# Turning the gated activations of a macaron block by transposing transfers instead of TensorE transposes

## The chip, the cores and the metric

The kernel runs on one core of one Trainium2 chip. The metric is the device time of one execution in microseconds (us). The engines are TensorE (PE, whose weight loads are listed apart as PEld), VectorE (DVE), ScalarE (ACT), GpSimd (POOL) and SyncE (SP, which only issues transfers here). Sixteen DMA engines move data for the queues of SP, POOL and ACT.

## The reference, cut to what matters

One layer of a streaming encoder, 256 tokens of 2048 features, all in float32. The residual stream passes through a first feed-forward, a recurrent middle part with two branches, a cross-attention and a second feed-forward, and a last norm:

```
x = x + 0.5 * swiglu(rms_norm(x, ffn1_norm), ffn1_w_up, ffn1_w_down)
...
x = x + 0.5 * swiglu(rms_norm(x, ffn2_norm), ffn2_w_up, ffn2_w_down)
return rms_norm(x, final_norm)

def swiglu(h, w_up, w_down):
    gate, up = jnp.split(h @ w_up, 2, axis=-1)
    return (jax.nn.silu(gate) * up) @ w_down
```

The change concerns only the two feed-forwards. The hidden width is 5632, so `w_up` has 11264 columns. `silu(gate) * up` is called the gated activations below.

## The kernel before, in words

**Numbers in two parts.** PE multiplies operands of a shortened float32 type. Each operand is therefore split into a high part, which ACT makes with a copy (line 155), and a low part, which DVE makes as the difference (line 156). A product is three matmuls: high by high (line 566), low by high (line 567) and high by low (line 569).

**The feed-forwards.** `ffn` works through 11 groups (g = 0 to 10) of 512 hidden features. A group is eight products ("steps") for the gate and up halves; most are of the kind "fast", in which seven accumulators in PSUM take products of sums and differences of weight blocks, 21 matmuls a step. In the second feed-forward every step is fast but the last two of group 0. When a group's products are done, ACT and DVE bring the seven accumulators together in two tiles of 128 partitions by 1024 (lines 653 to 665; `hid` and `hd` in the second feed-forward, one buffer each; the halves of a 2048 wide tile `ev` in the first). `activate` then makes the gated activations: ACT applies silu (line 599), DVE multiplies (line 600). They end in two blocks, `e0` for the first 128 tokens and `e3` for the other 128, tokens on partitions and 512 features along the row.

**The turn.** The down product needs them with features on partitions. `turn` (lines 602 to 613) takes eight blocks of 128 by 128 through PE (line 607, into two PSUM banks), and from each bank ACT copies a high part (line 611) and DVE makes a low part (line 612) into a tile `hidop`. `late` holds the calls that are to come later: a number n with each says after how many steps, the current one included, it is written into the program; `tick` counts at the end of every step. A turn is written with n = 4 (2 for g = 0).

**The order.** `ffn_order` gives the steps: the down products of two finished groups, four column blocks c of 512 for each, are mixed in behind the groups. Behind groups 1 and 2 stand two down products, behind each group from 3 on four, at the end eight for the groups 9 and 10. A down product of one c and one group is 24 matmuls, in two half steps of 12, one for each 128 tokens.

**What sets the order on the engines.** The kernel is written in one stream, and the framework's planner places each engine's instructions by its own costs and due times, so an engine can run an instruction somewhat earlier or later than it is written; where `issue_after` stands, not before a named one. Each engine then runs its own queue in order, and a waiting instruction holds all that stand behind it. Weight tiles are loaded by SP into `raw` buffers (lines 289 to 298), and prepared up to two steps ahead of use (`weights`, `prepare`); the high parts have three buffers of 2048 columns, and a fast step of the second feed-forward uses two of them. So ACT's split of a step's second tile waits until PE has let go of an earlier one.

**Other users of what the change touches.** `Operands.add` (line 397) makes the high and low parts of a normed block. The tile `hd` also serves as a throwaway output for the squares of the last norms (line 458), which come with the last down products.

Of the kernel before, what the change touches and what calls it, by code (L numbers as in the profile page):

```python
# [7 lines left out]

F32 = mybir.dt.float32
F32R = mybir.dt.float32r  # L10
ACT = mybir.ActivationFunctionType
ALU = mybir.AluOpType

P = 128
T = 256
# [46 lines left out]
def ffn_order(every=False):  # L62

    out = [("mixed" if p > 5 else "fast", 0, p) for p in range(8)] if every else first(0)
    down = [("down", 0, 1, c, 0) for c in range(4)]  # L70
    for g in range(1, NG):
        if every:
            out += [("fast", g, p) for p in (1, 3, 4, 0, 2, 5, 6, 7)]
        else:
            out += first(g)
        if g > 2 and g % 2:
            down = [("down", g - 2, 2, c, b) for c in range(4) for b in (g - 2, g - 1)]
        n = 2 if g < 3 else 4
        out, down = out + down[:n], down[n:]
    return out + [("down", NG - 2, 2, c, b) for c in range(4) for b in (NG - 2, NG - 1)]  # L80


def adds(name, e):
# [11 lines left out]
def block_kernel(ctx: ExitStack, tc: tile.TileContext, xT, xin, memT, vec, gfin, bgate, lruw, wu1, wd1, win, wv,  # L95
# [280 lines left out]
    class Operands:  # L376
# [13 lines left out]
        def add(self, src, gain=None):  # L390
            t = self.new()
            if gain is None:
                act.activation(t[:, :T], src, ACT.Copy)
                dve.tensor_tensor(out=t[:, T:], in0=src, in1=t[:, :T].bitcast(F32), op=ALU.subtract)
            else:
                act.activation(t[:, :T], src, ACT.Copy, scale=gain)
                dve.scalar_tensor_tensor(out=t[:, T:], in0=src, scalar=gain, in1=t[:, :T].bitcast(F32),
                                         op0=ALU.mult, op1=ALU.subtract)
            return t

# [89 lines left out]
    def turned(tile, which=range(2)):  # L490

        accs = [bank() for _ in which]
        for y, acc in zip(which, accs):
            for z in range(2):
                for t in range(2):
                    pe.transpose(acc[:, z * T + t * P:][:, :P], tile[:, t * 512 + (2 * y + z) * P:][:, :P], ident)  # L496
        return accs

    def normed(ops, c, gain):

        accs = turned(xt[c])
        for m in range(4):
            ops.add(accs[m // 2][:, m % 2 * T:][:, :T], col(gain, 4 * c + m))

# [77 lines left out]
    def ffn(name, pairs, sq, then, begin=(), sums=()):  # L584


        order = orders[name]
        uses = {}
        for e in order:
            if e[0] != "down":  # L590
                for i, (_, _, n) in enumerate(PRODUCTS[e[0]]):
                    uses.setdefault((e[1], n), []).append((e[2], i))
        hids, accs = {}, {}
        late = []
        rstd = None

        def activate(sg, gate, up, t):

            act.activation(sg, gate, ACT.Silu, scale=rstd[:, t:t + 1])
            dve.scalar_tensor_tensor(out=sg, in0=up, scalar=rstd[:, t:t + 1], in1=sg, op0=ALU.mult, op1=ALU.mult)  # L600

        def turn(g, hid):
            for y in range(2):
                acc = bank()
                for z in range(2):
                    for t in range(2):
                        pe.transpose(acc[:, z * T + t * P:][:, :P], hid[t][:, (2 * y + z) * P:][:, :P], ident)  # L607
                o = slot(F32R, "hidop")
                ov = o.rearrange("p (z s c) -> p z s c", z=2, s=2)
                av = acc.rearrange("p (z c) -> p z c", z=2)  # L610
                act.activation(ov[:, :, 0], av, ACT.Copy)
                dve.tensor_tensor(out=ov[:, :, 1], in0=av, in1=ov[:, :, 0].bitcast(F32), op=ALU.subtract)
                hids[2 * g + y] = o

        def tick():
            for i in range(len(late)):
                n, f = late.pop(0)
                if n > 1:
                    late.append((n - 1, f))
                else:  # L620
                    f()

        for at, e in enumerate(order):
            w = weights(name, *e)
            kind = e[0]
            following = order[at + 1][0] if at + 1 < len(order) else None
            if kind != "down":
                g, p = e[1:]
                fast = kind == "fast"
                products = []  # L630
                for i, (a, b, n) in enumerate(PRODUCTS["ready" if sums_ready(name, e) else kind]):
                    u = uses[g, n]
                    if u[0] == (p, i):
                        accs[n] = bank()
                    own, less = pairs[p]
                    products.append((accs[n], part(own, a, P) if a >= 0 else part(less, -1 - a, P), part(w[b // 4] if fast else w, b % 4, 512),
                                     u[0] == (p, i), u[-1] == (p, i)))
                three(products, 3 if adds(name, e) else 0, adds(name, e) and p == 6)
                last = at + 1 == len(order) or order[at + 1][1] != g or following == "down"
                ends = kind != "plain" and uses[g, 0][-1][0] == p  # L640
                if ends or last:
                    if ends or kind == "plain":
                        if "hid" in scoped:
                            ev = [scoped[n].tile([P, 1024], F32, name=n, tag=n) for n in ("hid", "hd")]
                            e0, e3, e1, e2 = (v[:, i:i + 512] for v in ev for i in (0, 512))
                        else:
                            ev = scoped["wide"].tile([P, 2048], F32, name="ev", tag="wide")
                            e0, e1, e2, e3 = (ev[:, i * 512:(i + 1) * 512] for i in range(4))
                        if rstd is None:
                            with tc.issue_after(done["high"]):  # L650
                                rstd = sq.rstd_tokens()
                if ends:
                    act.activation(e0, accs[0], ACT.Copy)
                    dve.tensor_tensor(out=e1, in0=accs[5], in1=e0, op=ALU.add)
                    dve.tensor_tensor(out=e2, in0=accs[4], in1=e1, op=ALU.add)
                if last:
                    if kind == "plain":
                        activate(e0, accs[0], accs[1], 0)
                        activate(e3, accs[3], accs[2], 1)
                    else:  # L660
                        for o, n, x in ((e0, 1, e0), (e1, 3, e1), (e1, 2, e1)):
                            dve.tensor_tensor(out=o, in0=accs[n], in1=x, op=ALU.add)
                        activate(e0, e0, e1, 0)
                        for o, n, x in ((e3, 6, e2), (e2, 3, e2)):
                            dve.tensor_tensor(out=o, in0=accs[n], in1=x, op=ALU.add)
                        activate(e3, e3, e2, 1)
                    late.append((4 if g else 2, lambda g=g, hid=(e0, e3): turn(g, hid)))
            else:
                first, n, c, block = e[1:]
                if block == first:  # L670
                    accs["down"] = [bank(), bank()]
                for t in range(2):
                    products = []
                    for k in range(4):
                        a = hids[2 * block + k // 2][:, k % 2 * 512:][:, :512]
                        products.append((accs["down"][t], (a[:, t * P:][:, :P], a[:, T + t * P:][:, :P]),
                                         part(w, k, 512), block == first and k == 0, block == first + n - 1 and k == 3))
                    three(products)
                    if block == first + n - 1:
                        o = xt[c][:, t * 512:(t + 1) * 512]  # L680
                        done["residual"] = dve.scalar_tensor_tensor(out=o, in0=accs["down"][t], scalar=0.5, in1=o,
                                                                    op0=ALU.mult, op1=ALU.add).ins
                        if block == NG - 1:
                            then(c, t)
            if sums:
                sums.pop(0)()
            if begin:
                begin.pop(0)()
            tick()


# [382 lines left out]
    late = []  # L1074
# [275 lines left out]
```

## Time and profile before

| | |
|---|---|
| median of 3 runs | 2417.07 us |
| lowest and highest | 2416.99 and 2417.82 us |
| profiled execution, its own time | 2418.76 us |
| its span | 2417.0 us |
| granted clock of PE | 0.999 |
| moved by the DMA engines | 684.33 MB |
| first feed-forward's last turn | at 642.2 us |
| second feed-forward's turns | from 1776.7 to 2359.3 us |

The profile is one execution on the chip. Its span runs from the first instruction to the last; the execution's own time is a little longer. Busy times are given for each engine with their share of the span. The page groups instructions by line, engine, operation and tiles; other views give the instructions of one stretch in order of time, busy times of a stretch, the waits by what ended them, and the chain of work that ended last, followed back from the end. In all of them a time is counted from the span's start.

### The profile page before, as it was taken

To read this page: it belongs to the slowest core of one execution; us is meant where nothing else is said; L and a number is where in the kernel's file an instruction comes from. 1 tells how busy PE (TensorE), PEld (TensorE's weight loads), DVE (VectorE), ACT (ScalarE), POOL (GpSimd) and SP (SyncE) were. 2 spreads that over 40 slices of the span, in tenths; PEclk is the share of its full clock that TensorE was granted. 3 is DMA by queue.
4 is the path that set the end of the run, shared out by engine and by line. 5 is a ranking of instruction groups with operands and counts; after the bars stand their busy time and mean duration, and the time that the engine had idled before them with its cause. 6 is when DMAs were issued, how large, how long until landed. Compare 5 with 4: busy or idle time off the path is not lost.

```text
span 2417.0 us, 30834 instructions
## 1 busy us (share of the span) xinstructions
PE 2405.1 (100%) x12116; PEld 2006.3 (83%) x12116; DVE 2044.6 (85%) x2275; ACT 1468.6 (61%) x1499; POOL 102.3 (4%) x166
## 2 busy tenths in 40 slices
PE   9999999999999999999999999999999999999998
PEld 8888888888888888888888888888888788888887
DVE  6999999999866878678876787777789999999995
ACT  8566777777654454476434555545676666666664
POOL 0000000000000000000000000000000000000000
PEclk9999999999999999999999999999999999999999
DMA  8578999999858776878989899876788877787773
GB/s 305 203 227 258 276 277 278 273 275 271 270 215 318 276 285 240 302 269 324 353 323 348 291 358 344 324 286 244 265 344 308 292 283 279 269 287 279 285 282 140
DMA packets 102386, 684.33 MB, mean 283 GB/s; under 512 B 11360, under 2 KB 11616, under 8 KB 29280
## 3 DMA queue, kind: packets, MB, share of 16 engines
q1 hardware_dynamic: 78192, 518.68, 57.5%
q0 software_dynamic: 23328, 162.54, 22.4%
q8 instruction: 95, 1.56, 0.2%
q10 hardware_dynamic: 720, 1.13, 0.1%
q14 instruction: 51, 0.42, 0.0%
HBM read 619.39 MB, written 62.91 MB: 282 GB/s over the span
## 4 chain that ended last, share of the span: by engine, by line
PE 97%; DVE 1%; ACT 1%; DMA 1%; issue 0%; ACTq 0%
PE acc L566 18%; PE acc L567 18%; PE acc L569 18%; PE acc L332 11%; PE acc L357 8%; PE acc L358 8%; PE acc L360 8%; PE acc L335 6%; PE acc L607 1%; PE acc L496 1%; ACT h L155 1%; DVE l L156 0%; PE acc L904 0%; DMA raw<-wd 0%; PE acc L1197 0%; PE acc L1151 0%
## 5 line engine op out<-in xcount | busy, mean ns | idle before, releaser
L155 ACT ACTIVATE h<-raw 128x2048 fp32r<-128x2048 f32 (+3 forms) x578 | 867.6, 1526 | 618.8 <-PE acc L358 209.5
L156 DVE TENSOR_TENSOR l<-raw,h 128x2048 fp32r<-128x2048 f32 (+2 forms) x406 | 833.8, 2056 | 209.3 <-ACT h L155 206.3
L566 PE MATMUL acc<-h,xh 128*128 128x512 f32 x1228 | 478.4, 392 | 0.5 <-ACT h L155 0.5
L567 PE MATMUL acc<-h,xl 128*128 128x512 f32 x1228 | 476.1, 390 | 0.0
L357 PE MATMUL acc<-h,ops 128*128 128x512 f32 x832 | 326.8, 393 | 0.0
L358 PE MATMUL acc<-h,ops 128*128 128x512 f32 x832 | 324.6, 390 | 0.0
L332 PE MATMUL acc<-ops,h 128*128 128x512 f32 x1152 | 278.0, 393 | 0.0
L566 PE MATMUL acc<-h,hidop 128*128 128x512 f32 x704 | 276.3, 392 | 1.5 <-ACT h L155 1.5
L566 PEld LDWEIGHTS acc<-h,xh 128*128 128x128 f32 x1228 | 230.5, 188 | 54.4 <-ACT h L155 6.2
L567 PE MATMUL acc<-h,hidop 128*128 128x512 f32 x704 | 274.4, 390 | 0.0
L567 PEld LDWEIGHTS acc<-h,xl 128*128 128x128 f32 x1228 | 230.6, 188 | 46.7
L332 PEld LDWEIGHTS acc<-ops,h 128*128 128x128 f32 x1152 | 211.6, 188 | 41.6
L156 DVE TENSOR_TENSOR tl<-raw,h 128x1024 fp32r<-128x1024 f32 x172 | 203.7, 1220 | 13.8 <-ACT h L155 13.3
L360 PE MATMUL acc<-l,ops 128*128 128x512 f32 x832 | 205.8, 389 | 0.0
L155 ACT ACTIVATE h<-td 128x1024 fp32r<-128x1024 f32 x140 | 146.6, 1055 | 82.6 <-DVE td L304 31.5
L569 PE MATMUL acc<-l,hidop 128*128 128x512 f32 x704 | 190.5, 389 | 0.0
L360 PEld LDWEIGHTS acc<-l,ops 128*128 128x128 f32 x832 | 156.2, 188 | 32.4
L357 PEld LDWEIGHTS acc<-h,ops 128*128 128x128 f32 x832 | 156.2, 188 | 32.3
L358 PEld LDWEIGHTS acc<-h,ops 128*128 128x128 f32 x832 | 156.3, 188 | 31.5
L569 PE MATMUL acc<-tl,xh 128*128 128x512 f32 x624 | 178.1, 392 | 0.1
L156 DVE TENSOR_TENSOR tl<-td,h 128x1024 fp32r<-128x1024 f32 x140 | 170.1, 1220 | 8.3 <-ACT h L155 7.4
L569 PE MATMUL acc<-l,xh 128*128 128x512 f32 x604 | 166.5, 390 | 0.0
(245 smaller groups left out, 2750.5 us busy)
## 6 DMA issues: line engine op xcount, KB each, us to landing
raw<-wu SPq DMA_DIRECT2D x114, 1024.0 KB, 6.3
raw<-wd SPq DMA_DIRECT2D x88, 1024.0 KB, 6.5
prep<-wu POOLq DMA_DIRECT2D x58, 1024.0 KB, 6.5
t<-prep POOLq DMA_DIRECT2D x58, 1024.0 KB, 5.7
raw<-t SPq DMA_DIRECT2D x58, 1024.0 KB, 7.1
raw<-wu SPq DMA_DIRECT2D x58, 768.0 KB, 4.8
raw<-win SPq DMA_DIRECT2D x40, 1024.0 KB, 4.9
raw<-wg SPq DMA_DIRECT2D x32, 1024.0 KB, 5.1
```

The lines of the kernel that those rows point to most:

```text
L155: done["high"] = act.activation(h, raw, ACT.Copy).ins
L156: done["low"] = dve.tensor_tensor(out=l, in0=raw, in1=h.bitcast(F32), op=ALU.subtract).ins
L332: pe.matmul(acc, h[:, k * P:(k + 1) * P], xs[k], start=k == 0, stop=False)
L335: done["product"] = pe.matmul(acc[:, :T], l[:, k * P:(k + 1) * P], xs[k][:, :T], start=False, stop=k == KT - 1).ins
L357: pe.matmul(accs[t], x[:, t * P:][:, :P], h[j], start=first and j == 0, stop=False)
L358: pe.matmul(accs[t], x[:, T + t * P:][:, :P], h[j], start=False, stop=False)
L360: done["product"] = pe.matmul(accs[t], x[:, t * P:][:, :P], l[j], start=False, stop=last and j == 3).ins
L496: pe.transpose(acc[:, z * T + t * P:][:, :P], tile[:, t * 512 + (2 * y + z) * P:][:, :P], ident)
L566: pe.matmul(acc, ah, bh, start=start, stop=False)
L567: pe.matmul(acc, al, bh, start=False, stop=False)
L569: pe.matmul(acc, ah, bl, start=False, stop=stop)
L607: pe.transpose(acc[:, z * T + t * P:][:, :P], hid[t][:, (2 * y + z) * P:][:, :P], ident)
```

## The change

The turn of twelve groups, all eleven of the second feed-forward and g = 10 of the first, no longer goes through PE. In its place stand three parts. `planes` is an ACT copy that treats the two blocks as 2048 16-bit numbers a partition and parts them: first all low halves, then all high halves. `across` is one transposing transfer, issued on ACT's queue, of the 128 by 2048 16-bit numbers: each 128 by 128 block is turned. It goes from the second tile back into the first. `turned_planes` is an ACT copy that joins the halves to float32 numbers in the second tile, and then the same high parts (ACT) and low parts (DVE) as in `turn`, read from that tile and not from PSUM. `planes` and `across` are written at the end of the group's last step (n = 1), `turned_planes` with n = 6. In the first feed-forward the order of the four blocks in `ev` changes, so that `e0` and `e3` lie side by side.

`Operands.add` gets a view of its tile with more dimensions; the bytes are the same. `normed` may take its blocks from a turn begun earlier, but `begun_turns` is empty here, and `begin_turn` and `end_turn` are not called.

```diff
+BY_DMA = {"ffn1": range(10, 11), "ffn2": range(0, 11)}
...
-                act.activation(t[:, :T], src, ACT.Copy, scale=gain)
-                dve.scalar_tensor_tensor(out=t[:, T:], in0=src, scalar=gain, in1=t[:, :T].bitcast(F32),
+                tv = t.rearrange("p (s t n) -> p s t n", s=2, t=2) if len(src.shape) > 2 else t.rearrange(
+                    "p (s n) -> p s n", s=2)
+                act.activation(tv[:, 0], src, ACT.Copy, scale=gain)
+                dve.scalar_tensor_tensor(out=tv[:, 1], in0=src, scalar=gain, in1=tv[:, 0].bitcast(F32),
...
+    def planes(a, b):
+
+        act.activation(b.bitcast(U16).rearrange("p (two n) -> p two n", two=2),
+                       a.bitcast(U16).rearrange("p (n two) -> p two n", two=2), ACT.Copy)
+
+    def across(a, b):
+
+        act.dma_start_transpose(a.bitcast(U16).rearrange("p (i n) -> p i n", n=P), b.bitcast(U16))
...
+        def turned_planes(g, a, b):
+            act.activation(b.bitcast(U16).rearrange("p (n two) -> p two n", two=2),
+                           a.bitcast(U16).rearrange("p (two n) -> p two n", two=2), ACT.Copy)
+            bv = b.rearrange("p (t k n) -> p k t n", t=2, k=4)
+            for y in range(2):
+                o = slot(F32R, "hidop")
+                ov = o.rearrange("p (z s t n) -> p z s t n", z=2, s=2, t=2)
+                act.activation(ov[:, :, 0], bv[:, 2 * y:2 * y + 2], ACT.Copy)
+                dve.tensor_tensor(out=ov[:, :, 1], in0=bv[:, 2 * y:2 * y + 2], in1=ov[:, :, 0].bitcast(F32),
+                                  op=ALU.subtract)
+                hids[2 * g + y] = o
...
-                            e0, e1, e2, e3 = (ev[:, i * 512:(i + 1) * 512] for i in range(4))
+                            e0, e3, e1, e2 = (ev[:, i * 512:(i + 1) * 512] for i in range(4))
+                            ev = ev[:, :1024], ev[:, 1024:]
...
-                    late.append((4 if g else 2, lambda g=g, hid=(e0, e3): turn(g, hid)))
+                    if g in BY_DMA[name]:
+                        late.append((1, lambda ev=ev: planes(*ev)))
+                        late.append((1, lambda ev=ev: across(*ev)))
+                        late.append((6, lambda g=g, ev=ev: turned_planes(g, *ev)))
+                    else:
+                        late.append((4 if g else 2, lambda g=g, hid=(e0, e3): turn(g, hid)))
```

More of the change, by code (lines that the diff above doesn't have):

```diff
@@ L10 @@
 F32R = mybir.dt.float32r
+U16 = mybir.dt.uint16
 ACT = mybir.ActivationFunctionType
@@ L497, in turned, with begin_turn, end_turn @@
         return accs
-    def normed(ops, c, gain):
-        accs = turned(xt[c])
+    def planes(a, b):
[3 more added lines that the diff above has]
+        act.dma_start_transpose(a.bitcast(U16).rearrange("p (i n) -> p i n", n=P), b.bitcast(U16))
+    def begin_turn(tile, free=False):
+        a = slot(name="planes")
+        b = tile if free else slot(name="across")
+        planes(tile, a)
+        across(b, a)
+        return b, a
+    def end_turn(b, a):
+        act.activation(a.bitcast(U16).rearrange("p (n two) -> p two n", two=2),
+                       b.bitcast(U16).rearrange("p (two n) -> p two n", two=2), ACT.Copy)
+        v = a.rearrange("p (t k n) -> p k t n", t=2, k=4)
+        return [v[:, k] for k in range(4)]
+    begun_turns = {}
+    def normed(ops, c, gain):
+        if gain in begun_turns:
+            parts = end_turn(*begun_turns.pop(gain))
+        else:
+            accs = turned(xt[c])
+            parts = [accs[m // 2][:, m % 2 * T:][:, :T].rearrange("p (t n) -> p t n", t=2) for m in range(4)]
         for m in range(4):
-            ops.add(accs[m // 2][:, m % 2 * T:][:, :T], col(gain, 4 * c + m))
+            ops.add(parts[m], col(gain, 4 * c + m))
     BOTH = [0, 2, 4, 6]
@@ L666, in ffn @@
                         activate(e3, e3, e2, 1)
-                    late.append((4 if g else 2, lambda g=g, hid=(e0, e3): turn(g, hid)))
+                    if g in BY_DMA[name]:
+                        late.append((1, lambda ev=ev: planes(*ev)))
+                        late.append((1, lambda ev=ev: across(*ev)))
+                        late.append((6, lambda g=g, ev=ev: turned_planes(g, *ev)))
+                    else:
+                        late.append((4 if g else 2, lambda g=g, hid=(e0, e3): turn(g, hid)))
             else:
```

## The prediction, made before the changed kernel was run

> **What bounds the kernel now.** I read the page's busy shares first, then the stretch of the second feed-forward in the windows view, then who PE waits for there, and last the chain of work.
>
> ```profile
> PE 2405.1 (100%) x12116; PEld 2006.3 (83%) x12116; DVE 2044.6 (85%) x2275; ACT 1468.6 (61%) x1499; POOL 102.3 (4%) x166
> ```
> ```profile
> 1780.00:2340.00 560.00, 557.92 (x2485) 458.20 (x2484) 515.66 (x479) 364.03 (x319) 6.07 (x7) 1.00 0.80 289
> ```
> ```profile
> PE acc L566 <- ACT h L155: 2.0, 3, 1.2
> ```
>
> The second row is one stretch: its length, then busy time of PE, PEld, DVE, ACT, POOL, then clock, DMA share and GB/s. PE is idle for 560.00 - 557.92 = 2.1 us of 560, and what it waits for (third row, from 1680 us to the end) is the split of a weight tile into its high part by ACT. The reader is to see two things. Every PE instruction taken away shortens this stretch at once. And the engines behind PE have little to give: DVE is busy for 516 of 560 us, ACT for 364, the DMA engines for 0.80.
>
> **What the change removes.** Twelve groups (g = 10 of the first feed-forward, all eleven of the second) lose their eight PE transposes each.
>
> ```profile
> 642.35 0.87 PE acc L607 x8
> ```
> ```profile
> 1987.90 0.91 PE acc L569 x4
> 1990.62 0.91 PE acc L569 x4
> 1994.23 0.91 PE acc L569 x4
> 1996.95 0.91 PE acc L569 x4
> 2001.03 1.59 PE acc L569 x7
> 2005.79 1.59 PE acc L569 x7
> 2366.62 0.91 PE acc L569 x4
> 2369.34 0.91 PE acc L569 x4
> ```
>
> In the chain one turn takes 0.87 us. The second fence gives the same: the half steps of the down products end 2.72 us apart (1987.90 to 1990.62), and 3.61 us apart where the turn lies between them. So PE is relieved of 12 x 0.87 = **10.4 us**, all of it on the path. Each turn also frees two PSUM banks; PE's waits name no bank, so I count nothing for that.
>
> **What it adds on ACT and DVE.** Per group: one copy that parts the 16-bit halves (2048 elements a partition), one transfer issued on ACT's queue, one copy that joins the halves (2048 again), and the two operand copies and two DVE differences as before, from SBUF and not from PSUM.
>
> ```profile
> L273 ACT ACTIVATE l<-raw 128x2048 fp32r<-128x2048 f32 x18 | 34.3, 1907 | 2.0 <-PE acc L569 2.0
> L611 ACT ACTIVATE hidop<-acc 128x512 fp32r<-128x512 f32 x44 | 24.0, 587 | 3.8 <-PE acc L607 3.6
> L155 ACT ACTIVATE xh<-xg 128x512 fp32r<-128x512 f32 x16 | 10.1, 634 | 0.4
> L612 DVE TENSOR_TENSOR hidop<-acc,hidop 128x512 fp32r<-128x512 f32 x44 | 28.6, 684 | 0.9 <-ACT hidop L611 0.7
> L156 DVE TENSOR_TENSOR xl<-xg,xh 128x512 fp32r<-128x512 f32 x16 | 10.9, 689 | 12.4 <-ACT xh L155 12.4
> ```
>
> No row shows a 16-bit copy. ACT's 128x2048 copy takes 1.9 us; 16-bit elements could halve that (0.95) or the stride could double it (3.8); I take 1.9, the row with the same count. The operand copy moves from 587 to 634 ns, the DVE difference from 684 to 689: nothing. ACT gains 2 x 1.9 + 0.1 = 3.9 us a group, 47 us in all, on an engine that is busy 61% of the time. The view strides in the norm's operand helper name the same bytes as before: nothing.
>
> **Where that lies.** ACT runs its queue in order, so what stands behind the new instructions matters. This is ACT and DVE at the end of an ordinary group (bracket: idle before it), with the windows of the same place:
>
> ```profile
> 1981.60 1.31 ACT L599 ACTIVATE hid<-hid,rtok 128x512 f32<-128x512 f32 x2
> 1985.27 1.49 ACT L155 ACTIVATE h<-raw 128x1536 fp32r<-128x1536 f32 x1 [2.35 <-issue]
> 1990.70 2.01 ACT L155 ACTIVATE h<-raw 128x1024 fp32r<-128x1024 f32 x2 [3.95 <-PE acc L567]
> 1992.62 1.07 ACT L611 ACTIVATE hidop<-acc 128x512 fp32r<-128x512 f32 x2
> 1997.04 1.49 ACT L155 ACTIVATE h<-raw 128x1536 fp32r<-128x1536 f32 x1 [3.35 <-issue]
> 2004.02 3.39 ACT L155 ACTIVATE h<-raw 128x1024 fp32r<-128x1024 f32 x3 [1.37 <-PE acc L567]
> ```
> ```profile
> 1982.61 1.41 DVE L600 SCALAR_TENSOR_TENSOR hid<-hd,rtok,hid 128x512 f32<-128x512 f32 x2
> ```
> ```profile
> 1984.00:1998.00 14.00, 14.00 (x68) 11.68 (x67) 9.34 (x11) 5.43 (x6) 0.00 (x0) 1.00 1.00 347
> 1998.00:2030.00 32.00, 32.00 (x143) 26.48 (x142) 31.65 (x27) 22.16 (x20) 0.00 (x0) 1.00 0.66 241
> 2045.00:2106.00 61.00, 61.00 (x274) 50.06 (x273) 57.21 (x55) 39.37 (x34) 0.87 (x1) 1.00 0.77 271
> ```
>
> The new wait: the halves can be parted only when DVE's L600 has ended, at 1984.0. ACT stood idle from 1982.9 to 1985.3 anyway. Parting runs to 1985.9, the issue follows. Behind it are queued the split at 1985.27 and the pair at 1990.70, for products that start at 1996.95 + 0.91 = 1997.86 (after the change about 1997.0). The first split takes 1.49, the pair 2.01, and the pair is used six matmuls (6 x 0.227 = 1.36) later: ACT must be back by 1998.36 - 3.50 = 1994.9. **That is 8.5 us of room after the issue at about 1986.4.** ACT is busy for only 5.4 of these 14 us, and 1.07 of that, the operand copies, moves out.
>
> The joining copy is written after the first product of the next group, which ends about 1997.0 + 4.76 (2001.03 to 2005.79) = 2001.8. There ACT has 1.37 us idle in each 4.76 us product. The 1.9 + 1.27 us bunched there (before: 1.07, elsewhere) are made up within three products; the pair that they push back has 1.36 us of the product's start and the idle 1.37 for cover. Without that cover it would be up to 0.5 us a group. DVE is the tighter engine: 31.65 busy of 32. What ACT withholds from it for longer than DVE's idle 3.8 us in a group (61.00 - 57.21), PE pays.
>
> **The transfer.** 512 KB from SBUF to SBUF, its issue and its landing. No transposing transfer is in the trace.
>
> ```profile
> 1986.24 0.33 SPq L294 DMA_DIRECT2D raw<-wu  x1
> ```
> ```profile
> bgate<-bgate SPq DMA_DIRECT2D x4, 512.0 KB, 6.1
> mem<-memT SPq DMA_DIRECT2D x4, 512.0 KB, 9.7
> ```
> ```profile
> l<-wd POOLq DMA_DIRECT2D x1, 1024.0 KB, 13.0
> ```
>
> An issue costs 0.33 us in SP's row; landing takes 6.1 to 9.7 us for this size, and 13.0 us for the slowest transfer between 1984 and 2045 (last row). The windows say why the upper end counts: in the 14 us behind a group's end the DMA share is 1.00. I take 0.5 us for the issue and 8 us to land: 1994.4, and 1999.4 at 13 us, both before the joining copy wants it (2001.8). ACT's queue is behind neither SP's nor POOL's, but all three share the engines: 512 KB at the 347 GB/s of that window is 1.5 us of all engines, so the weight loads there slip by about that. The next window, at 0.66, takes it up.
>
> The Trainium skill speaks against the change: "VectorE: DVE Perf Modes", section "The three transpose paths", gives 390 ns for a 128x128 16-bit transpose on TensorE and 1309 ns by transfer. By it sixteen blocks, one after another, would be an estimated 21 us and land near 2007, after the joining copy wants it: the late form of the second rival. This case's TensorE row, 0.87 us for eight in a stream, is far below its 390 ns each, so by this trace its figures fit single operations, not a stream of them, and I give the late form a quarter of that rival's chance.
>
> **The last groups.** There the operands are wanted soonest.
>
> ```profile
> 2349.61 1.40 DVE L600 SCALAR_TENSOR_TENSOR hid<-hd,rtok,hid 128x512 f32<-128x512 f32 x2
> ```
>
> Ready at 2351.0; parted 2352.9, issued 2353.4, landed 2361.4 (2366.4 at 13 us), joined, copied and first difference made 1.9 + 0.63 + 0.69 = 3.2 us later: 2364.6 (2369.6). Wanted when the tenth half step ends, 2369.34 + 0.91 - 0.87 = 2369.4. Hidden, at the upper end just not. The first feed-forward's last group has the same shape.
>
> **The sum.** 10.4 us gained. ACT's 47 us, the transfers and their waits are hidden where I can place them. For the small slips I take as much as PE already waits in that stretch, 2.1 us; bounds 0 and 5 (0.5 a group). Net 8.3 us. The profiled execution took 2418.76 us round its span of 2417.0; it is 1.7 above the median 2417.07. From it: 2410.5; from the median: **2408.8 us**.
>
> **Rivals.**
> 1. *The gain is given back* (no change). DVE at 57.2 of 61 us becomes the bound in each group: ACT's bunched copies starve it and PE then waits for a low part. For it: the 31.65 of 32. Against it: DVE idles 4.7 us in the 14 us before, just where most of ACT's new work lies. At 0.9 us a group over ten groups: 2417.07 - 10.4 + 9 = about 2416.
> 2. *ACT's queue is held by the transfer* (slower), at the issue while its descriptors wait for saturated DMA engines, or at the joining copy because it lands late. Place: behind each group's end. It decides from 8.5 us of holding; beyond that PE stands one for one. If ACT comes back only when the engines are free, at 1998, that is 3.1 us a group, and over the ten groups 0 to 9: 2417.07 - 10.4 + 31 = about 2438. Groups 0 to 2 have fewer or no down products behind them and would pay more. If it is only late at the joining copy, say after twice the slower row of its size, 2 x 9.7 = 19.4 us, it lands at 2005.8; ACT stands 4.0 us, of which 1.37 + 1.36 are covered: 1.3 us a group, 2417.07 - 10.4 + 13 = about 2420. For it: DMA share 1.00 there, and no row for such a transfer. Against it: the issue of a weight load into that same window is 0.33 us in SP's row, and 13 us still lands in time.
>
> **Chances.** Forecast 0.60, rival 1 0.15, rival 2 0.25. What a measurement of this kernel can tell from no change is about 0.2%, 4.8 us: 2412.2 to 2421.9. A little of rival 1 falls below 2412.2: faster 0.62, same 0.13, slower 0.25. Low end: the whole 10.4 and a little PSUM ease, 2405. High end into rival 2, halfway between its two forms, 2429; beyond that 0.16 is left out, below 2405 0.03. The forecast's own range is 2405 to 2412.
>
> **What would show it.** PE's instructions fall from 12116 to 12020 and the L607 group from 176 to 80. ACT's busy time rises by about 47 us: a rise of 23 or 94 would show the 16-bit copies mis-sized. An ACT queue with twelve transposing transfers appears; median landing above 15 us, or ACT idle for over 8.5 us behind them, speaks for rival 2. PE's idle time between 1780 and 2340 rising from 2.1 to about 11 us would be rival 1, with DVE named as releaser. I am wrong if PE's waits for L155 grow by more than 5 us.

## The result, and the profile after

The changed kernel takes **2558.23 us** (median of 4 runs, 2552.32 to 2567.66) against 2417.23 us for the kernel before beside it (4 runs, 2416.99 to 2417.82): a ratio of 1.0587 [1.0551, 1.0622], 141 us slower. The profiled execution took 2561.84 us round a span of 2560.0. In the changed kernel's lines, the split of weights is L159 and L160 (before L155, L156), the three matmuls are L602, L603 and L605 (before L566, L567, L569), and the turn through PE is L643. New are L507 (parting copy), L512 (transposing transfer), L652 (joining copy), L658 and L659 (operand copies and differences).

The page of the changed kernel: span, busy times, packets, ACT's queue (q10: packets, MB, share of 16 engines), chain by engine.

```profile
span 2560.0 us, 30659 instructions
...
PE 2428.5 (95%) x12020; PEld 2010.2 (79%) x12020; DVE 2043.5 (80%) x2275; ACT 1516.8 (59%) x1523; POOL 102.3 (4%) x166
...
DMA packets 127345, 690.60 MB, mean 270 GB/s; under 512 B 36320, under 2 KB 36576, under 8 KB 54240
...
q10 hardware_dynamic: 25680, 7.43, 3.2%
...
PE 72%; DMA 12%; DVE 8%; ACT 5%; issue 3%; DVEq 0%; ACTq 0%; SPq 0%
```

PE has lost its 96 transposes (12116 to 12020), but the span has grown by 143.0 us. That splits in two: PE stands for 2560.0 - 2428.5 = 131.5 us, 119.6 more than before (2417.0 - 2405.1 = 11.9), and it is *busy* for 23.4 us more, with fewer instructions. The chain names who is waited for: DMA has 12% of it. The page before has q10 with 720 packets and 11360 packets under 512 B; now there are 24,960 more of both, 2080 small packets for each of the twelve transfers (0.52 MB, so some 250 B each).

The stretch of the second feed-forward that the prediction showed, in the windows view of the changed kernel:

```profile
1780.00:2340.00 560.00, 478.52 (x2006) 382.92 (x2005) 429.40 (x402) 340.14 (x286) 5.22 (x6) 0.93 0.83 250
```

PE was busy for 557.92 of these 560 us; now it is idle for 81. All of PE, DVE and ACT do less in the same time, and the DMA engines are busier (0.83 for 0.80) but move less (250 GB/s for 289). Who waits for whom, over the whole run of the changed kernel (total, times, longest):

```profile
PEld acc L602 <- ACT h L159: 114.9, 52, 20.3
...
PE acc L602 <- ACT h L159: 96.6, 24, 19.9
...
ACT hd L652 <- DMA hid<-hd: 80.3, 10, 19.2
...
ACT h L159 <- issue: 62.0, 15, 11.3
```

PE waits for ACT's weight splits (96.6 us against 2.0); ACT in turn stands at the joining copy until the transfer has landed, and at the issue. The total of that last row has not grown (69.8 us in 26 waits before), only its longest wait, from 3.5 us to 11.3. One group (g = 5), on ACT's timeline of the changed kernel (ACTq is ACT's sequencer, which issues the transfer):

```profile
2101.47 1.91 ACT L507 ACTIVATE hd<-hid 128x2048 uint16<-128x2048 uint16 x1 [1.47 <-DVE hid L636]
2103.29 1.47 ACT L159 ACTIVATE h<-raw 128x1536 fp32r<-128x1536 f32 x1
2103.41 9.36 ACTq L512 DMA_TRANSPOSE hid<-hd  x1
2112.89 2.01 ACT L159 ACTIVATE h<-raw 128x1024 fp32r<-128x1024 f32 x2 [8.13 <-issue]
2134.11 2.48 ACT L652 ACTIVATE hd<-hid 128x2048 uint16<-128x2048 uint16 x1 [19.21 <-DMA hid<-hd]
...
2137.68 3.36 ACT L159 ACTIVATE h<-raw 128x1536 fp32r<-128x1536 f32 x3
```

The issue holds ACT's queue for 9.36 us, not 0.5. The planner has put the joining copy only two places behind it, with one pair of splits between. There ACT stands for 19.21 us, and behind it stand the next weight splits. Over all groups, the tile's view and the transfer's landing in the changed kernel:

```profile
L512 ACTq DMA_TRANSPOSE hid<-hd x11: 1902/8921/16497, 1795.1 to 2490.4; - x11
...
DMA to landing us min/median/max: 6.8/17.2/31.8
```

The hold is 1.9, 8.9 and 16.5 us (least, median, most). The landing after 30.7 us in the group shown is one of the long ones; the median is 17.2. The last piece of the reading is what the transfer does to the loads beside it. The DMA view of that group's 31 us (103 to 134 us behind 2000) in the changed kernel:

```profile
q1 hardware_dynamic: 480, 3.20, 65.2%
q10 hardware_dynamic: 2080, 0.52, 28.2%
...
raw<-t SPq DMA_DIRECT2D x1, 1024.0 KB, 24.3
raw<-wu SPq DMA_DIRECT2D x1, 1024.0 KB, 19.0
raw<-wu SPq DMA_DIRECT2D x1, 768.0 KB, 19.8
hid<-hd ACTq DMA_TRANSPOSE x1, 30.7
```

SP's weight loads, 5.4 to 7.1 us over the run, took 19 to 24 us here. So the wait has two candidate causes. **Theory A**, the prediction's second rival: ACT's queue is held, at the issue and at the join. **Theory B**: the small packets of one queue and the large packets of another share the DMA engines badly, so the transfer and the loads are both late, and PE would starve even if ACT never stood. What the operation costs on engines alone (the copies) is a third.

### The profile page after: what moved, and what is told of

The parts are those of the page before. It is cut to its first block, busy times and chain, and to the rows that moved or that the text cites. A ratio compares the mean times of both kernels' runs of the same rounds, so it can differ in the third digit from the quotient of the medians.

```text
span 2560.0 us, 30659 instructions
## 1 busy us (share of the span) xinstructions
PE 2428.5 (95%) x12020; PEld 2010.2 (79%) x12020; DVE 2043.5 (80%) x2275; ACT 1516.8 (59%) x1523; POOL 102.3 (4%) x166
## 2 busy tenths in 40 slices
DMA packets 127345, 690.60 MB, mean 270 GB/s; under 512 B 36320, under 2 KB 36576, under 8 KB 54240
## 3 DMA queue, kind: packets, MB, share of 16 engines
q10 hardware_dynamic: 25680, 7.43, 3.2%
## 4 chain that ended last, share of the span: by engine, by line
PE 72%; DMA 12%; DVE 8%; ACT 5%; issue 3%; DVEq 0%; ACTq 0%; SPq 0%
PE acc L602 10%; PE acc L336 10%; PE acc L603 10%; PE acc L605 10%; DMA hid<-hd 7%; PE acc L361 7%; PE acc L362 7%; PE acc L364 7%; PE acc L339 5%; DVE tl L160 3%; ACT h L159 2%; DMA raw<-wd 2%; DVE l L160 2%; DMA raw<-t 1%; DMA ev<-ev 1%
## 5 line engine op out<-in xcount | busy, mean ns | idle before, releaser
L159 ACT ACTIVATE h<-raw 128x2048 fp32r<-128x2048 f32 (+3 forms) x578 | 865.2, 1525 | 607.5 <-PE acc L362 202.1
L160 DVE TENSOR_TENSOR l<-raw,h 128x2048 fp32r<-128x2048 f32 (+2 forms) x406 | 833.0, 2055 | 224.4 <-ACT h L159 222.4
L602 PE MATMUL acc<-h,xh 128*128 128x512 f32 x1228 | 490.4, 402 | 97.2 <-ACT h L159 94.2
L603 PE MATMUL acc<-h,xl 128*128 128x512 f32 x1228 | 484.5, 397 | 0.0
L602 PEld LDWEIGHTS acc<-h,xh 128*128 128x128 f32 x1228 | 235.8, 192 | 163.5 <-ACT h L159 109.7
L602 PE MATMUL acc<-h,hidop 128*128 128x512 f32 x704 | 279.2, 397 | 19.0 <-ACT hidop L658 16.4
L603 PE MATMUL acc<-h,hidop 128*128 128x512 f32 x704 | 277.7, 394 | 0.0
L603 PEld LDWEIGHTS acc<-h,xl 128*128 128x128 f32 x1228 | 236.1, 192 | 48.0
L160 DVE TENSOR_TENSOR tl<-raw,h 128x1024 fp32r<-128x1024 f32 x172 | 203.1, 1217 | 55.2 <-ACT h L159 55.2
L605 PE MATMUL acc<-l,hidop 128*128 128x512 f32 x704 | 193.1, 394 | 4.3 <-DMA l<-wd 3.5
L159 ACT ACTIVATE h<-td 128x1024 fp32r<-128x1024 f32 x140 | 146.6, 1054 | 82.2 <-DVE td L308 27.9
L605 PE MATMUL acc<-tl,xh 128*128 128x512 f32 x624 | 180.0, 393 | 1.5 <-DVE tl L160 1.4
L160 DVE TENSOR_TENSOR tl<-td,h 128x1024 fp32r<-128x1024 f32 x140 | 169.8, 1218 | 9.6 <-ACT h L159 8.8
L602 PEld LDWEIGHTS acc<-h,hidop 128*128 128x128 f32 x704 | 134.1, 190 | 49.9 <-ACT hidop L658 17.3
```

What stands on the lines that cost most here:

```text
L159: done["high"] = act.activation(h, raw, ACT.Copy).ins
L160: done["low"] = dve.tensor_tensor(out=l, in0=raw, in1=h.bitcast(F32), op=ALU.subtract).ins
L602: pe.matmul(acc, ah, bh, start=start, stop=False)
L603: pe.matmul(acc, al, bh, start=False, stop=False)
L605: pe.matmul(acc, ah, bl, start=False, stop=stop)
```

## The experiments

Each stands beside runs of the kernel before on the same chip: 2417.89, 2417.45 and 2418.21 us in the three sets (1 to 4, 5 to 8, 9 to 12).

**1. The copies alone.** `across` is not called; the join reads the parted tile.

```diff
-                        late.append((1, lambda ev=ev: across(*ev)))
-                        late.append((6, lambda g=g, ev=ev: turned_planes(g, *ev)))
+                        late.append((6, lambda g=g, ev=ev: turned_planes(g, ev[1], ev[0])))
```

> The transfer is left out, the two 16-bit copies stay: the halves are parted into the second tile and joined back into the first, so the activations are not turned (part of the computation left out). Theory (the transfer costs it all, by holding ACT's queue): 2407 to 2411 us, the forecast without the transfer. Rival (ACT's added 3.9 to 4.4 us a group starve DVE): over 2417, up to 2558.

Measured: 2412.70 us (2411.83 to 2414.28), 0.9977 [0.9967, 0.9987], a little above the 2407 to 2411 of the theory. Without the transfer nothing is lost, and 5 us are gained. All that the change loses comes with the transfer and its waits; ACT's 48 us of copies are hidden.

**2. The same bytes, not transposed.** A plain transfer of the same tile on the same queue.

```diff
-        act.dma_start_transpose(a.bitcast(U16).rearrange("p (i n) -> p i n", n=P), b.bitcast(U16))
+        act.dma_start(a.bitcast(U16), b.bitcast(U16))
```

> A plain transfer of the same 512 KB from the second tile to the first, on ACT's queue, in place of the transposing one (so nothing is turned). Theory (it is the transposing transfer's 2080 small packets): 2408 to 2420 us, landing 4 to 9 us. Rival (any 512 KB on ACT's queue at this place, while the DMA engines are saturated, holds it): over 2500.

Measured: 2424.77 us (2421.24 to 2426.35), 1.0025 [1.0016, 1.0034], above the 2408 to 2420 expected and far from the rival's 2500. The DMA view, the queue and the join's wait:

```profile
hid<-hd ACTq DMA_DIRECT2D x11, 512.0 KB, 8.1
```
```profile
ACT hd L652 <- DMA hid<-hd: 17.1, 8, 3.4
```

The prediction's 8 us to land is right for a plain transfer. Even that comes a little late where the planner joins: 17.1 us of waiting. It costs 12 us over the copies alone; the transposing form costs 146.

**3. The transfer aside.** PE turns as before the change; the parting copy and the transposing transfer on ACT's queue run too, behind PE's turn, and nobody uses their result.

```diff
-                        late.append((1, lambda ev=ev: across(*ev)))
-                        late.append((6, lambda g=g, ev=ev: turned_planes(g, *ev)))
+                        late.append((3, lambda g=g, ev=ev, hid=(e0, e3): (turn(g, hid), across(*ev))))
```

> TensorE turns as before (written at n = 3), the halves are parted, and the transposing transfer is issued on ACT's queue right behind the turn, but nothing reads its result. So the issue's hold on ACT and the load on the DMA engines stay, the wait for the landing goes. If the wait at the join were all (95 us of ACT's waits): 2417 to 2425. If the hold at the issue (median 8.9 us) and the slowed weight loads carry part of it: 2440 to 2520.

Measured: 2479.49 us (2470.38 to 2493.92), 1.0257 [1.0220, 1.0295]: 62 us with no wait at the join. One instruction still waited for a landing: a later user of the buffer of `ev`, on DVE (last fence; PE's longest wait from then to 720 us was 6 us). The profiled execution is the slowest of the four, 2493.92 us. From 1780 us to the end, in ACT's waits:

```profile
ACT h L159 <- issue: 35.1, 5, 9.6
ACT h L159 <- DMA raw<-t: 31.0, 8, 14.0
...
ACT h L159 <- DMA raw<-wu: 21.8, 5, 11.8
```
```profile
DVE S L937 <- DMA ev<-ev: 16.5, 1, 16.5
```

ACT has five waits of up to 9.6 us at the issue (before: 15 of up to 3.5 us, 42.7 in all), and it stands for 53 us because these weight tiles have not come (10.7 before, from 1680 us on). So not the join alone is at fault. Both theories have a row here.

**4. The transfer on SP's queue**, where the weight loads are.

```diff
-        act.dma_start_transpose(a.bitcast(U16).rearrange("p (i n) -> p i n", n=P), b.bitcast(U16))
+        sp.dma_start_transpose(a.bitcast(U16).rearrange("p (i n) -> p i n", n=P), b.bitcast(U16))
```

> As the changed kernel, but SP issues the transposing transfers, so the hold at the issue falls on the weight loads' queue and not on ACT. If the hold on ACT is the main cost: 2430 to 2490, with ACT free behind the parting copy. If the late landing at the join, or the slowed weight loads, are the main cost: 2540 to 2600.

Measured: 2435.33 us (2433.59 to 2438.27), 1.0067 [1.0050, 1.0083]. One word takes back 123 of the 141 us. The DMA view and the tile's view of this kernel:

```profile
hid<-hd SPq DMA_TRANSPOSE x11, 7.2
```
```profile
L512 SPq DMA_TRANSPOSE hid<-hd x11: 1692/5105/6841, 1780.8 to 2376.3; - x11
```

ACT is no longer held, as theory A wants. But the same transfer also lands in 7.2 us instead of 17.2, which A does not explain: it now stands in one line with the loads. The next set separates the two.

**5. ACT's queue, but the join late.** The join is written at n = 8 (6 in the last group), and `issue_after` holds it behind the latest split, so that the planner can't put it forward.

```diff
-                        late.append((6, lambda g=g, ev=ev: turned_planes(g, *ev)))
+                        def join(g=g, ev=ev):
+                            with tc.issue_after(done["high"]):
+                                turned_planes(g, *ev)
+                        late.append((8 if g < NG - 1 else 6, join))
```

> As the changed kernel (transfer on ACT's queue), but the joining copy is written at n = 8 (6 for the last group) and kept behind ACT's newest weight split, so that ACT reaches it some ten instructions after the issue instead of two. Its 95 us of waits for the landing should fall below 15. If that wait was the cost: 2412 to 2425. If the hold at the issue and the weight loads slowed by sharing the DMA engines carry most of it, as in the run where nobody read the result (2479): 2455 to 2500.

Measured: 2513.13 us (2504.8 to 2522.39), 1.0403 [1.0374, 1.0431], above both ranges. Waits of this kernel:

```profile
DVE raw L308 <- DMA raw<-wu: 37.4, 8, 14.6
...
ACT ev L652 <- DMA ev<-ev: 22.5, 1, 22.5
...
ACT hd L652 <- DMA hid<-hd: 2.1, 1, 2.1
```

The second feed-forward's wait at the join is gone (80.3 to 2.1 us), and only 45 us of the 141 come back. Other waits take its place: DVE now stands for weight loads, and the one join of the first feed-forward stands for 22.5 us.

**6. SP's queue and the join late** (edits 4 and 5 together).

> SP issues the transfers, and the joining copy is late as in the run before this one. On SP's queue the transfer landed in 7.2 us, and ACT waited 38.8 us for it at the join. If that early join is what is left of the loss (2435): 2410 to 2419. If it is the weight loads that stand behind the transfer on SP's queue: 2428 to 2438 again.

Measured: 2430.37 us (2429.02 to 2434.91), 1.0054 [1.0041, 1.0067], 5 us below experiment 4, but the intervals overlap; it is still 13 over before.

**7. The test of theory B.** As 6, with ACT never held, but the *weight loads* of the second feed-forward move to POOL's queue, so that transfer and loads are in different queues again. **8** is its control: the kernel before with the loads moved in the same way.

```diff
+    def loader():
+        return nc.gpsimd if "raw2" in scoped else sp
...
-            sp.dma_start(raw, src)
+            loader().dma_start(raw, src)
...
```

> SP issues the transfers (join late as before), but in the second feed-forward the weight loads go to POOL's queue, so that transposing packets and load packets again come from two queues while ACT is never held at an issue. Against the next kernel, which has the same loads and TensorE's turns. If two queues on the DMA engines are the cause: landing over 12 us and 20 us or more slower than the next kernel. If it was only the hold on ACT: landing near 7 us and within 6 us of the next kernel.

> The kernel before, with the second feed-forward's weight loads on POOL's queue: the control of the run before this one. 2415 to 2440, since POOL takes about 0.87 us an issue and its queue also waits for ACT ahead of each accumulating load.

Measured: 7 takes 2514.49 us (2509.2 to 2521.33), 1.0400 [1.0384, 1.0417]; 8 takes 2425.63 us (2423.04 to 2425.88), 1.0030 [1.0019, 1.0041]. In 7, the DMA view and DVE's wait for loads:

```profile
hid<-hd SPq DMA_TRANSPOSE x11, 20.3
...
ev<-ev SPq DMA_TRANSPOSE x1, 7.1
```
```profile
DVE raw L312 <- DMA raw<-wu: 61.1, 9, 13.7
```

This decides between the queue and ACT's hold. With the loads in the other queue the turn costs 2514.49 - 2425.63 = 89 us, with the loads in its own queue 13 (experiment 6), and in neither is ACT's queue held by an issue. One kernel even shows both: `hid` (loads elsewhere) lands in 20.3 us, `ev` of the first feed-forward (loads in the same queue) in 7.1. On ACT's queue with the same late join it was 2513.13 - 2417.45 = 96 us. The 7 us between 96 and 89 are no more than the runs of either kernel spread, so ACT's hold at the issue costs little or nothing that these runs show. Theory B stands for the largest part, A for the join that the planner put too early (45 us, experiment 5).

The packet records of the traces add what the loads meet there. A load packet of 4 KB or more takes 0.31 us (median). From 1750 us on, none takes over 2.5 us in the kernel before or wherever the transfer is plain, left out, or in the loads' own queue. In the four kernels in which a transposing transfer stands in another queue than the loads, 83 to 146 of them do, up to 7.8 us: 146 in the changed kernel, and 83, 116 and 114 in experiments 3, 5 and 7.

**9. Small packets without transposing.** Two plain transfers a turn on ACT's queue, in runs of 256 bytes; joined accordingly (not shown). In all 25680 packets on q10, as in the changed kernel.

```diff
-        act.dma_start_transpose(a.bitcast(U16).rearrange("p (i n) -> p i n", n=P), b.bitcast(U16))
+        for i in range(2):
+            act.dma_start(a.bitcast(U16).rearrange("p (m two n) -> p m two n", two=2, n=P)[:, :, i],
+                          b.bitcast(U16)[:, i * 1024:(i + 1) * 1024].rearrange("p (m n) -> p m n", n=P))
```

> As the run with a plain transfer on ACT's queue (2425), but the 512 KB go as two transfers in runs of 256 bytes, the packet size of the transposing transfer: about 2048 small packets, nothing turned. If small packets that alternate with the 8 KB packets of the loads' queue are the cause: landing over 12 us, 2480 to 2560. If it is the transposing itself: 2420 to 2440.

Measured: 2489.77 us (2484.67 to 2492.02), 1.0295 [1.0281, 1.0309]. The page's queue, the tile's view, the landing and the join's wait:

```profile
q10 hardware_dynamic: 25680, 7.43, 1.3%
```
```profile
L513 ACTq DMA_DIRECT2D hid<-hd x22: 601/636/1223, 1787.1 to 2416.7; - x22
```
```profile
hid<-hd ACTq DMA_DIRECT2D x22, 256.0 KB, 10.6
```
```profile
ACT hd L654 <- DMA hid<-hd: 78.5, 10, 15.2
```

The same bytes on the same queue as experiment 2, and 65 us slower, by the packet size and one more issue a turn. The time is in the range expected for small packets; the landing, 10.6 us for each half, stays below the 12 that I expected with it. An issue holds ACT for 0.64 us, yet the join waits as long as in the changed kernel (78.5 and 80.3 us). The other 68 us up to 2558 come with the transposing form. Part of that is plain in the share of q10: 3.2% of 16 engines for 1.3%, that is (3.2% x 2560.0 - 1.3% x 2489.9) / 12 = 4.1 us more of all sixteen engines for each transfer.

**10. SP's queue, the transfer written later** (n = 5) and the join at n = 8: to move the transfer out of the 14 us in which the DMA engines are full.

```diff
-                        late.append((1, lambda ev=ev: across(*ev)))
+                        late.append((5 if g < NG - 1 else 1, lambda ev=ev: across(*ev)))
```

> SP issues the transfers and the join is late (2430 so far); the transfer is now written at n = 5 (1 for the last group), behind the 14 us in which the DMA engines are saturated. If the loads that it pushes back in that stretch are what is left of the loss: 2412 to 2422. If not: 2426 to 2435.

Measured: 2433.98 us (2431.92 to 2434.51), 1.0066 [1.0053, 1.0079]. The first range failed: this other place gains nothing over experiment 6. The diff shows only what differs from that experiment.

**11. The copies alone, joined late** (1 and 5 together).

> No transfer (as in the first run, 2412.7, so nothing is turned), but the joining copy late, at n = 8. If the first run's missing 5 us came from the joining copy standing among the splits: 2407 to 2410. If ACT's 3.9 to 4.4 us a group cost it wherever they stand: 2411 to 2414.

Measured: 2422.61 us (2419.70 to 2425.94), 1.0017 [1.0009, 1.0026]: 10 us *worse* than with the join where the planner put it. It lies above both of my ranges. A late join costs some 10 us in itself; I read this as its 2.5 us and the operand copies standing between other splits, but no run shows it by itself (PE's waits for the splits grow from 3.7 us in experiment 1 to 7.0). It stands 4 us over before, and experiments 6 and 10 stand 8 and 11 us above it: that is what the transfer still costs in SP's queue, and its cause stays open. Neither place of the join is good there: the early one waits for the landing (38.8 us of ACT in experiment 4), the late one has its own cost.

**12. Nothing at all**: neither copies nor transfer, operands straight from the unturned activations. It gives the ceiling for a turn that costs nothing, with the operand copies where they are.

> Neither 16-bit copies nor transfer: the operands are made straight from the unturned activations (the turn left out). It measures the term of the sum that the change takes away: 10.4 us, so 2406 to 2408. More or less would show that term mis-sized.

Measured: 2412.86 us (2411.16 to 2414.34), 0.9980 [0.9971, 0.9989]. Its page and its waits over the run:

```profile
PE 2395.3 (99%) x12020; PEld 1996.1 (83%) x12020; DVE 2043.1 (85%) x2275; ACT 1468.9 (61%) x1499; POOL 102.3 (4%) x166
```
```profile
PEld acc L602 <- ACT h L159: 14.8, 29, 1.8
...
PE acc L602 <- ACT h L159: 5.2, 7, 1.4
```

PE's busy time falls by 9.8 us, as the twelve turns promise, but its idle time rises from 11.9 to 2411.6 - 2395.3 = 16.3: 4.4 us come back, 3.2 of them named as PE's waits for weight splits (2.0 to 5.2 us). So a free turn is worth 5.3 us here, and with experiment 1 the copies cost nothing. The ceiling is 5 us; the best placing of a real transfer is 13 us over before.

## Why the prediction was wrong

**The step that failed** is the transfer: "I take 0.5 us for the issue and 8 us to land", with the weight loads that "slip by about that", 1.5 us. Measured on ACT's queue beside the loads: the issue held the queue for 8.9 us (median, up to 16.5), the transfer landed after 17.2 us (up to 31.8), and loads beside it took 19 to 24 us. I sized the transfer by its bytes (512 KB, 1.5 us of all engines), from rows of plain transfers (those of its size land in 5.9 to 9.7 us, not 6.1 to 9.7, which changes nothing). By bytes it is still 1.1% of what the kernel moves (7.43 of 690.60 MB); by packets it is a fifth (25680 of 127345), and packets are what the queues took turns by.

The DMA view shows how. Two short windows of one transfer of the changed kernel (g = 4), 2042 to 2045 us while loads are queued, and 2048 to 2050 when they have paused:

```profile
q1 hardware_dynamic: 206, 1.20, 95.6%
q10 hardware_dynamic: 204, 0.05, 7.7%
```
```profile
q10 hardware_dynamic: 1243, 0.31, 69.8%
```

The packets of the two queues come one for one (206 to 204; in the groups g = 6 and 8, 260 to 265 and 256 to 255 in 4 us). While loads are waiting the transfer gets 68 packets a microsecond, and 2080 would take it 31 us; alone it gets over 600. In one queue with the loads there are no two queues to take turns, and it lands after 7.2 us. The Trainium skill has this rule, in "DMA: Bandwidth & Descriptors", section "Queues, rings and completion order": each DMA engine takes the queues that have work in turn, a packet at a time. The trace agrees in the equal counts, and I had not weighed it. (The page has several descriptors to a packet; no run here shows whether a packet of the profile is one of these.)

**Where the join stands.** "Written after the first product of the next group", 2001.8 in the old times, some 15 us behind the issue: what the planner did was to put it on ACT two places behind the issue, with one pair of splits between. I had written in front that the planner may run an instruction earlier than it is written, and then took the written place. Even with 8 us to land (experiment 2) ACT waited 17.1 us there, and the kernel took 12 us more than without a transfer.

**The second rival** had the place and the sign right, and both of its forms appear: an issue held and a join late. Its prices were 31 and 13 us, from "ACT comes back only when the engines are free", 1998, and 19.4 us to land. The hold was priced at 11.6 us (1986.4 to 1998) and measured at 8.9, beside a room of 8.5; it is the small part, 7 us or less where the join is late. The late join was priced for the written place; from the planner's place the 17.2 us to land cost far more. What the rival missed is that the loads are late as well; with the join late, DVE stands for them for up to 14.6 us at a time (experiment 5; 13.7 in 7). Its chance was also booked askew: the late form at 2420 lies inside the prediction's own "same", 2412.2 to 2421.9, but all of the rival's 0.25 went to "slower".

**A second term missed**: PE is busy for 23.4 us more with 96 instructions fewer. Less the 9.8 us of the turns, that is 33 us more for the matmuls. The windows of the group shown above (g = 5), and the end of its stall on PE's timeline:

```profile
2118.00:2123.00 5.00, 1.34 (x6) 0.75 (x4) 0.00 (x0) 0.00 (x0) 0.00 (x0) 1.00 1.10 89
2123.00:2128.00 5.00, 0.00 (x0) 0.00 (x0) 0.00 (x0) 0.00 (x0) 0.00 (x0) 0.52 1.50 106
2128.00:2134.10 6.10, 0.00 (x0) 0.00 (x0) 0.00 (x0) 0.00 (x0) 0.00 (x0) 0.50 0.34 118
```
```profile
2139.20 0.80 PE L602 MATMUL acc<-h,xh 128*128 128x512 f32 x1 [19.86 <-ACT h L159]
2139.79 0.63 PE L603 MATMUL acc<-h,xl 128*128 128x512 f32 x1
...
2144.11 0.39 PE L602 MATMUL acc<-h,xh 128*128 128x512 f32 x1
2144.34 0.40 PE L603 MATMUL acc<-h,xl 128*128 128x512 f32 x1
```

PE's last matmul before the stall ends at 2119.3. The granted clock (column before the last two) is 1.00 up to 2123.2 and then 0.5, and after the stall matmuls start 0.43 us apart for 4.4 us, until about 2143.6, then 0.23 apart again. A long stall thus costs some 2 us on top of itself. The Trainium skill describes it in "TensorE: Matmul & The Clock Gate", Part 1: half the clock after an idle window of about 3.4 us, the full one after as much work. The trace agrees within about a microsecond (3.9 and 4.4 us). In all, the trace has eleven stretches at half clock before the end, with 49.2 us of busy PE in them; half of that, 25 us, is my estimate of what the clock took. The other 8 us came without it: experiment 4, at a clock of 0.999, has 8.1 us more of busy PE than experiment 12 (2403.4 and 2395.3).

**The gain was half what I took**: "10.4 us, all of it on the path" is 9.8 off PE's busy time and 5.3 off the time. What failed in the reading is "Every PE instruction taken away shortens this stretch at once": part of the gain turned into waits for weight splits. The first rival had a gain given back, but named DVE, ACT's bunched copies and the low parts; the waits name ACT's high parts, and they grow without any copies (experiment 12).

**Right** were the count of instructions; ACT's gain, 47 us predicted and 1516.8 - 1468.6 = 48.2 measured; and that it is hidden (experiments 1 and 12 differ by 0.2 us). Its two terms, predicted at 1.9 us each, in the changed kernel (busy time and mean ns before the last column):

```profile
L652 ACT ACTIVATE hd<-hid 128x2048 uint16<-128x2048 uint16 x11 | 27.5, 2502 | 80.3 <-DMA hid<-hd 80.3
...
L507 ACT ACTIVATE hd<-hid 128x2048 uint16<-128x2048 uint16 x11 | 21.0, 1908 | 10.3 <-DVE hid L636 10.2
```

Parting is 1.91 us, joining 2.50. So here a 16-bit copy with a strided read takes as long as the 32-bit one of the same count (1.91 us), and the one with a strided write 0.6 us longer. Of the marks that the prediction set, the landing over 15 us and PE's waits for the weight splits grown by over 5 us both came true.

## What to carry to other kernels

Price a transfer by its packets and its queue, not by its bytes alone: a transfer of many small packets that runs beside large loads belongs in the queue of those loads, where the transposing one cost 13 to 17 us here and not 89 to 141 (plain small packets in the loads' queue were not tried). Before you move work from a busy engine to a transfer, take the work out altogether for one run: here that showed a ceiling of 5 us, and no transfer tried here left any of it over. And read on the engine's timeline where the planner really puts a waiting instruction, since everything behind it waits too.

## What was not expected of the hardware, and what stays open

The twelve transposing transfers are 24,960 packets of some 250 bytes. Their issue holds the issuing engine's queue for 1.7 to 6.8 us on SP's queue with the loads (experiment 4), for 1.9 to 15.9 on SP's queue with the loads elsewhere (7), and for 1.9 to 16.5 on ACT's; the plain transfers in 256-byte runs hold it for 0.64 us (median).

The Trainium skill says in "DMA: Bandwidth & Descriptors", section "Issuing engines are not separate DMA queues", that issuing from several engines saves only the time to issue. Here the choice of the issuing engine is worth 123 us (experiment 4 against the changed kernel), and the measurement decides; by experiment 7 it is not the engine that counts but whether the loads stand in the same queue.

Open is why the landings alternate: for groups 3 to 9 they are 26.0, 13.2, 30.7, 12.3, 31.8, 13 and 29.2 us. The long ones are not only a matter of taking turns. In the 31 us shown above a packet of the loads took 65.2% x 16 x 31 / 480 = 0.67 us on average, and one of the transfer 0.067; in the two short windows it was 0.22 and 0.018. The packet records say where the loads' average comes from: 31 of the 480 took over 2.5 us each and 176 of the 324 us together, while the median was 0.31. The long landings of groups 3, 5, 7 and 9 have 26 to 31 such packets each, the short ones of 4, 6 and 8 none, and experiment 9 none at all. (Groups 0 and 1 have 16 and 15.) So they belong to a transposing transfer beside loads in another queue, but what held these packets, and why in every other group, no run shows. With it stays open how the 68 us beyond experiment 9 divide: the held load packets, the longer packets of the transfer (4.1 us of all engines a transfer) and the held issue weren't tried apart.
